# A two-branch encoder layer on one core: when branch B's token copies are made, how branch B's outputs lie in DRAM, and which engine makes the low parts of h's sums

## The chip, the cores and the metric

The kernel runs on one core of a Trainium2 chip. The core has a matrix engine (PE, TensorE; its weight loads are listed apart as PEld), a vector engine (DVE, VectorE), an activation engine (ACT, ScalarE), a general engine (POOL, GpSimd) and a queue that issues the DMAs (SP, SyncE). Each engine works off its own list of instructions in order; semaphores hold one back until its inputs are there. The metric is device time of one execution, in microseconds, as the median of several executions.

## The reference

An encoder layer with two parallel gated branches is applied to two requests with shared weights: a prompt of 512 tokens and a sample of 1024 tokens, 1024 channels each.

```python
h = rmsnorm(x, norm_g)
qa, ka, va, za, qb, kb, vb, zb, ga, gb = split(h @ w_in)
oa = neighbourhood_attention(rmsnorm(qa), rmsnorm(ka), va, rpb_a) * silu(za) @ w_o_a
ob = window_gqa_attention(rmsnorm(qb), rmsnorm(kb), vb, t5_table, sink) * silu(zb) @ w_o_b
y = x + (sigmoid(ga) * oa + sigmoid(gb) * ob) @ w_out
```

Branch A attends on a grid of 64 columns, 8 heads. Branch B attends to tokens at most 128 positions away, with 8 query heads on 2 key heads. All is in float32.

## The kernel before

**Precision.** Every operand of a large product is split in two parts for PE: a high part (ACT copies it into float32r) and a low part (the operand less its high part, on DVE or POOL). A product is then three matmuls: high by high, high by low, low by high (L1293 to L1295; L764 in the projections). The function split (L1168) makes both parts: the high part with ACT alone (L1172), the low part (L1177) with the choice any_tt, DVE or POOL.

**Stages.** For each request: norm, attention (attention_phase, L651), then the dense part (dense_phase, L1139): the paths z_a and z_b, the gates, the two branch projections and the output projection. The prompt runs first and the sample second; the sample's norm lies beside the prompt's dense part. In the trace the prompt's attention takes up to about 220 us, its dense part to about 400, the sample's attention to about 785 and its dense part the rest.

**The planner.** The kernel is first written as a list of operations, each with the engines that may do it and a price per engine, a due number (prio; small is early), the buffers that it needs, and the operations after which it comes. Flow.run (L207) then walks through time with these prices, gives each free engine the ready operation of the smallest due number, and so writes down each engine's order. An operation that DVE and POOL may both do is also marked port (L170): the planner starts it on one of them only when the other has no port operation running (barred, L252). The DMAs are priced by bytes alone (dma, L188). On the chip the engines follow these orders, and semaphores keep data right.

**Attention.** Tokens lie column by column of the grid. Branch A has four groups of two heads, branch B two groups of four; in each, project (L731) makes q, k and v of 128 tokens at a time (4 tiles in the prompt, 8 in the sample), with due number lead + t, lead being the group times the tiles. For branch B a tile is every nb-th token (nb = 4 or 8), so its operand is first copied together: hb, four copies of 128 x 512 for a tile (L751 to L757; ACT L665, DVE L667), in four buffers (HB). They are due one before their tile, and wait for all of h. f.begun (L775) holds the first matmul of each projection. Then sums of squares (ss, L788), rs_v and rs_r on POOL (L795, L802), the scaled q and k (qk, L819), transposes on PE (L864), scores, weights and outputs ot.

**Branch outputs.** Outputs go to DRAM (o_d, L404) and are read back when the path z is there (post_z, L1524). For branch B an output tile ot has 128 partitions: two parts e of 64 channels each, which the reader adds (L1540). Its store (L1098 to L1107) is two DMAs, one for each e: 64 partitions in runs of 128 tokens (512 B). The tokens of a row stand tile after tile in DRAM. The sample's reader takes a half of the tokens (L1532), so 64 tokens out of each of eight tiles, in runs of 256 B; the prompt's reader takes a whole row of 2 KB.

**Dense part.** Pairs of output blocks are made with sums of h and sums of weights (one level of Strassen's scheme, pair_strassen L1349), seven products in place of eight. The sample's sums of h are stored in DRAM (t_d) and loaded by stored_sums (L1236): sixteen tiles of 128 x 512, split into the tiles T. The same function loads the later sums of the merged branches (m_d). weight_tiles (L1260) splits the weights: whi by ACT, wlo by DVE or POOL; S are the sums of weights. The first z pair of a request has prio 0, the later ones 1 to 3. Filled gate products (fill_gates, L1592; fh, fl, fc, tile d) are put where PE has room.

Of the kernel before, what the change touches and what calls it, by code (L numbers as in the profile page):

```python
# [10 lines left out]
F32 = mybir.dt.float32  # L11
# [14 lines left out]
FILL_P, FILL_S = 3, 8  # L26
SLACK = 1.1
SCRATCH = 1024
CLASSIC_P = (4, 8, 4)
# [11 lines left out]
P = 128  # L41
# [313 lines left out]
def encoder_kernel(  # L355
# [23 lines left out]
    nc = tc.nc  # L379
# [23 lines left out]
    t_d = dpool.tile([4, 4, P, NT_S // 2], F32, tag="t_d", name="t_d")  # L403
    o_d = {geo.nt: dpool.tile([2, 8, P, geo.nt], F32, tag=f"o_d{geo.nt}", name=f"o_d{geo.nt}") for geo in (gp, gs)}  # L404

# [245 lines left out]
    def attention_phase(geo, hh, hl, h_ops, mask_d, early, late):  # L651
# [79 lines left out]
        def project(br, w, t, prio):  # L731
# [5 lines left out]
            if br == "A":  # L737
                hs = h_ops[t]
                part = [lambda k, v=v: v.t[:, k, t * P : (t + 1) * P] for v in (hh, hl)]
                held = [[hh] * KC, [hl] * KC]  # L740
                done = {}
            else:

                hs = []
                hb = [[tile_([P, KC // 2, P], F32R, "hb", HB) for _ in range(2)] for _ in range(2)]
                part = [lambda k, v=v: v[k // 4].t[:, k % 4] for v in hb]
                held = [[v[k // 4] for k in range(KC)] for v in hb]
                done = {}
                for q in range(2):
                    for m, v in enumerate((hh, hl)):  # L750
                        done[m, q] = f.op(  # L751
                            (("act", 960), ("dve", DVE_(512))),
                            lambda e, m=m, v=v, q=q: copy(
                                e, hb[m][q].t, v.t[:, 4 * q : 4 * q + 4, t:nt:nb].bitcast(F32)
                            ),
                            prio - 1, new=[hb[m][q]], hold=[v], after=[o for u in h_ops.values() for o in u], port=True,
                        )  # L757
# [79 lines left out]
        def over(v, runs):  # L837

            (a, n), b = runs[0], runs[-1][0]
            return v[:, a : a + n] if len(runs) == 1 else v.rearrange("p (a b) -> p a b", b=n)[:, a // n :: (b - a) // n]  # L840
# [120 lines left out]
        def weigh(br, gi, g, block, sums, pss, sbs, nb_t, info, prio):  # L961
# [114 lines left out]
            if br == "A":  # L1076
# [10 lines left out]
                def emit():  # L1087
                    if len(runs) == 1:
                        dst = over(o_d[nt][0, g], runs).rearrange("(i p) n -> p i n", i=2)
                        nc.sync.dma_start(dst, ot.t[:64, ::2])  # L1090
                        return
                    for i in range(2):
                        dst = over(o_d[nt][0, g, 64 * i : 64 * i + 64], runs)
                        nc.sync.dma_start(dst, ot.t[:64, 2 * i].rearrange("p (a b) -> p a b", b=64))

                stores[g, runs[0][0] // 512].append(sp(emit, 65536, prio, use=[ot]))
            else:
                for e in range(2):  # L1098
                    dst = o_d[nt][e, 4 + 2 * g : 6 + 2 * g, :, runs[0][0] : runs[0][0] + P]
                    dst = dst.rearrange("c (i d) n -> d (c i) n", d=64)  # L1100
                    o = sp(
                        lambda e=e, dst=dst: nc.sync.dma_start(dst, ot.t[e * 64 : e * 64 + 64]),
                        131072, prio, use=[ot],
                    )
                    for c in (4 + 2 * g, 5 + 2 * g):
                        for n in range(nt // 512):
                            stores[c, n].append(o)  # L1107

# [30 lines left out]
    def dense_phase(geo, hh, hl, h_ops, o_stores, exps_done, start, opened, tp, up, p0, p1, p2, x_t, y_t, classic, fill, after_gates=None, side=None):  # L1139
# [27 lines left out]

        def split(hi, lo, src, n, prio, new_hi, new_lo, src_v, after=()):  # L1168

# [5 lines left out]
            b = f.op(  # L1175
                any_tt(n),
                lambda e: engines[e].tensor_tensor(lo(), src(), hi().bitcast(F32), op=ALU.subtract), prio,  # L1177
# [58 lines left out]
        def stored_sums(prio, d, after):  # L1236

            tv, ops = {}, {}
            for j in (1, 2, 0, 3):
                tv[j] = tuple(f.value(tp, [P, 4, nh], F32R, "T", 8) for _ in range(2))  # L1240
                vh, vl = tv[j]
                for k in range(4):
# [6 lines left out]
                        lambda vh=vh, k=k: vh.t[:, k], lambda vl=vl, k=k: vl.t[:, k], lambda st=st: st.t[:, :nh], nh, prio,  # L1249
                        (vh, k == 0), (vl, k == 0), [st],  # L1250
                    )
# [7 lines left out]

        def weight_tiles(operands, per, prio):  # L1260

# [4 lines left out]
            for i, src in enumerate(operands):  # L1266
                at, q = [], 0
                while q < 4:
# [6 lines left out]
                        lambda src=src, sc=sc: src.t[:, sc], m * P, prio,  # L1275
                        (hi, ti not in seen), (lo, ti not in seen), [src],
                    )
# [71 lines left out]
        def pair_strassen(srcs, post, prio, mov_h, mov_t, seed=None, last=False, kept=None):  # L1349
# [10 lines left out]
            first = [] if kept else [raw[0, 0], raw[0, 1]]  # L1360
            w = weight_tiles([*first, s2, s3, s1, raw[1, 1], s4], 6, prio - 0.5)
            w = [None] * (7 - len(w)) + w
# [161 lines left out]
        def post_z(c, a, n, v, in_psum, prio):  # L1524
# [3 lines left out]
            for e, ot in enumerate(ots):  # L1528
                if c < 4:
                    src, dst = o_d[nt][e, c, :, a : a + n], lambda ot=ot: ot.t[:, :n]  # L1530
                else:
                    src = o_d[nt][e, c].rearrange("p (i n) -> p i n", n=P)[:, :, a // nb : a // nb + m]  # L1532
                    dst = lambda ot=ot: ot.t[:, :n].rearrange("p (i n) -> p i n", n=m)
                dma(
                    lambda dst=dst, src=src: nc.sync.dma_start(dst(), src), 512 * n, prio - 0.5, new=[ot],
                    after=o_stores[c, a // nh],
                )
# [416 lines left out]
```

## Time and profile before

| | us |
|---|---|
| median of 3 runs | 1136.02 |
| lowest and highest of them | 1134.59, 1136.24 |
| the profiled execution, as timed | 1135.29 |
| its span, first to last instruction | 1133.5 |

| engine | busy in the prompt's attention at 100 to 120 us | in the sample's attention at 500 to 520 | in the sample's dense part at 900 to 920 |
|---|---|---|---|
| PE | 20.00 | 20.00 | 20.00 |
| DVE | 15.98 | 16.23 | 13.12 |
| ACT | 16.82 | 12.21 | 7.94 |
| POOL | 8.98 | 12.38 | 6.32 |

Each stretch is 20 us long. Busy is the time in which an instruction of that engine runs; of the matmuls the ends are modelled, and consecutive ones overlap, so a PE that is busy throughout can still hold fewer matmuls than fit. The number of matmuls of a stretch therefore says more than its busy time. In the views an operation is named by its line, its engine and out<-in by the program's names; what stands behind an arrow is what ended the idle time ahead of it.

### The profile page before, as it was taken

The page shows a single profiled execution, that of the slowest core. Times are in us where ns is not written, and L with a number is a line of the kernel's source. Part 1 is how long each engine was busy: PE and PEld are TensorE (multiplying, and loading weights), DVE is VectorE, ACT ScalarE, POOL GpSimd, SP SyncE. Part 2 cuts the span into 40 slices and gives each one's busy share as a digit, 9 for nine tenths or more (in the row PEclk, how much of TensorE's full clock was granted, in tenths as well). Part 3 has the DMA queues.
Part 4 walks back from the last instruction along what each step waited for, and adds up shares of the span by engine and source line. Part 5 has one row for each costly group of instructions (what it writes and reads, how often), then busy time and mean ns, then how long its engine had stood idle before and what let it go on. Part 6 is the DMA issues. An engine that isn't in the chain of part 4 may idle for free.

```text
span 1133.5 us, 18690 instructions
## 1 busy us (share of the span) xinstructions
PE 1119.0 (99%) x6079; PEld 973.2 (86%) x6079; DVE 860.1 (76%) x1988; ACT 651.9 (58%) x1499; POOL 337.3 (30%) x438
## 2 busy tenths in 40 slices
PE   8999999999999999999999999999999999999998
PEld 6999988888888889999999988988788888888887
DVE  5888797587776568787878888885988766677764
ACT  6777987644432257565769888876543335423430
POOL 4653433000011154434324344420333322222211
PEclk9999999999999999999999999999999999999999
DMA  7854543488886732121212314244977645867862
GB/s 263 276 155 138 184 115 103 110 257 248 256 278 216 254 128 91 27 63 30 82 41 85 81 38 112 57 131 121 307 241 234 224 156 170 281 207 222 280 215 93
DMA packets 139108, 186.11 MB, mean 164 GB/s; under 512 B 29897, under 2 KB 68561, under 8 KB 139010
## 3 DMA queue, kind: packets, MB, share of 16 engines
q1 hardware_dynamic: 139010, 184.91, 51.8%
q8 instruction: 48, 0.79, 0.3%
q14 instruction: 50, 0.41, 0.1%
HBM read 137.66 MB, written 51.92 MB: 167 GB/s over the span
## 4 chain that ended last, share of the span: by engine, by line
PE 93%; DMA 2%; DVE 2%; issue 1%; ACT 1%; POOL 1%; SPq 0%; DVEq 0%; ACTq 0%
PE p L764 25%; PE x L1294 9%; PE x L1295 9%; PE x L1293 9%; PE x L1066 5%; PE x L937 5%; PE x L1029 5%; PE d L1293 4%; PE d L1295 4%; PE d L1294 4%; PE p L1294 4%; PE p L1295 4%; PE p L1293 4%; PE x L864 2%; DMA w<-in_w_att_dram 1%
## 5 line engine op out<-in xcount | busy, mean ns | idle before, releaser
L764 PE MATMUL p<-whi,hh 128*128 128x384 f32 x384 | 133.4, 348 | 0.0
L764 PE MATMUL p<-whi,hl 128*128 128x384 f32 x384 | 132.2, 344 | 0.0
L764 PE MATMUL p<-wlo,hh 128*128 128x384 f32 x384 | 131.8, 343 | 0.0
L1172 ACT ACTIVATE whi<-raw 128x512 fp32r<-128x512 f32 (+1 forms) x140 | 81.4, 600 | 71.2 <-PE x L1294 22.3
L981 ACT ACTIVATE sb<-sb,mx 128x384 f32<-128x384 f32 (+1 forms) x192 | 107.8, 565 | 16.9 <-DVE mx L972 16.5
L1295 PE MATMUL x<-T,wlo 128*128 128x512 f32 x280 | 108.9, 389 | 0.0
L1294 PE MATMUL x<-T,whi 128*128 128x512 f32 x280 | 108.9, 389 | 0.0
L1293 PE MATMUL x<-T,whi 128*128 128x512 f32 x280 | 108.9, 389 | 0.0
L764 PE MATMUL p<-whi,hb 128*128 128x384 f32 x384 | 107.6, 346 | 0.0
L1177 POOL TENSOR_TENSOR wlo<-raw,whi 128x512 fp32r<-128x512 f32 (+1 forms) x33 | 39.5, 1204 | 215.6 <-DMA raw<-in_w_g_dram 112.9
L1040 DVE TENSOR_TENSOR pp<-x,pp 128x512 fp32r<-128x512 f32 (+1 forms) x136 | 82.5, 638 | 19.6 <-ACT pp L1035 19.0
L1177 DVE TENSOR_TENSOR wlo<-raw,whi 128x512 fp32r<-128x512 f32 (+1 forms) x107 | 72.0, 682 | 32.3 <-ACT whi L1172 28.7
L802 POOL TENSOR_TENSOR rs_r<-rs_v,mhalf 128x4 f32<-128x4 f32 (+1 forms) x72 | 80.5, 1118 | 5.7
L1035 ACT ACTIVATE pp<-x 128x512 fp32r<-128x512 f32 (+1 forms) x136 | 70.8, 559 | 15.8 <-PE x L1029 14.3
L1294 PE MATMUL x<-hl,whi 128*128 128x512 f32 x200 | 77.8, 389 | 0.0
L1295 PE MATMUL x<-hh,wlo 128*128 128x512 f32 x200 | 77.8, 389 | 0.0
L1293 PE MATMUL x<-hh,whi 128*128 128x512 f32 x200 | 77.8, 389 | 0.0
L1066 PE MATMUL x<-pp,v 128*128 128x256 f32 (+1 forms) x368 | 75.8, 322 | 0.0
L764 PEld LDWEIGHTS p<-whi,hl 128*128 128x128 f32 x384 | 72.6, 189 | 1.3 <-issue 1.0
L764 PEld LDWEIGHTS p<-wlo,hh 128*128 128x128 f32 x384 | 72.7, 189 | 1.0 <-issue 0.7
L764 PEld LDWEIGHTS p<-whi,hh 128*128 128x128 f32 x384 | 72.7, 189 | 0.7 <-DVE v L812 0.3
L764 PEld LDWEIGHTS p<-whi,hb 128*128 128x128 f32 x384 | 69.1, 188 | 3.1 <-issue 1.3
(388 smaller groups left out, 2965.1 us busy)
## 6 DMA issues: line engine op xcount, KB each, us to landing
raw<-in_w_g_dram SPq DMA_DIRECT2D x84, 256.0 KB
w<-in_w_att_dram SPq DMA_DIRECT2D x46, 384.0 KB
raw<-in_w_z_dram SPq DMA_DIRECT2D x40, 256.0 KB
ot<-o_d SPq DMA_DIRECT2D x36, 256.0 KB
g_d<-C SPq DMA_DIRECT2D x34, 256.0 KB
fr<-in_w_g_dram SPq DMA_DIRECT2D x28, 256.0 KB
raw<-in_w_out_dram SPq DMA_DIRECT2D x28, 256.0 KB
out_dram<-C SPq DMA_DIRECT2D x19, 256.0 KB
```

What stands on the lines that cost most here:

```text
L764: pe.matmul(ps.t[:, :GW], part[u](k), mv.t[:, c], start=k == 0 and m == 0, stop=k == KC - 1 and m == 2,)
L802: lambda e: nc.gpsimd.tensor_tensor(r.t[:, :nn], rv.t[:, :nn], mhalf[:, :nn], op=ALU.pow),
L937: pe.matmul(pss[2 * pair + i].t[:, :width], q.t[rows, u, at : at + P], kv[:, tiles[0] : tiles[-1] + 1 : step], start=n == 0, stop=n == 2,)
L981: act.activation(sb.t[:, :width], sb.t[:, :width], AF.Exp, bias=mx.t[:, i : i + 1], scale=-1.0, accum_out=sm.t[:, i : i + 1],)
L1035: lambda e, pt=pt, pp=pp, nn=nn: act.activation(pp.t[:, 0, :nn], pt.t[:, :nn], AF.Copy),
L1040: lambda e, pt=pt, pp=pp, nn=nn: dve.tensor_tensor(pp.t[:, 1, :nn], pt.t[:, :nn], pp.t[:, 0, :nn].bitcast(F32), op=ALU.subtract),
L1066: pe.matmul(out(), v.t[:, vs], mv(), start=first, stop=last)
L1172: (("act", ACT_(n)),), lambda e: act.activation(hi(), src(), AF.Copy), prio,
L1177: lambda e: engines[e].tensor_tensor(lo(), src(), hi().bitcast(F32), op=ALU.subtract), prio,
L1293: pe.matmul(out, hi.t[:, cs], mh(), start=first and k == 0, stop=False, **more)
L1294: pe.matmul(out, hi.t[:, cs], ml(), start=False, stop=False, **more)
L1295: pe.matmul(out, lo.t[:, cs], mh(), start=False, stop=last and k == len(ws) - 1, **more)
```

## The change

Three things change. First, the copies hb of branch B's tokens also come after the first matmul of the projection six tiles back (AHEAD). Second, branch A's outputs keep o_d, now without the part e, and branch B's get a tensor of their own, ob_d: for each half of 512 tokens, eight blocks of 128 rows. A store takes all 128 partitions of ot for one half (two DMAs in the sample, with 64 tokens of a row each; one in the prompt, with 128), and a reader takes rows of 512 tokens. Third, split has a switch, both: where it is off, the low part has DVE alone. It is off for the sums of h that the sample loads (stored_sums with t_d), and for the weights of a Strassen pair with prio 0.

```diff
@@ -25,6 +25,7 @@
 ROTA = "ppxxxxxd"
 FILL_P, FILL_S = 3, 8
 SLACK = 1.1
+AHEAD = 6
 SCRATCH = 1024
 CLASSIC_P = (4, 8, 4)
 SIDE = {5: 0, 8: 1, 11: 2, 15: 3}
@@ -401,7 +402,8 @@
         rpb_x[geo.nt] = dpool.tile([8, P, 3 * geo.cw * 16], F32, tag=f"rpb_x{geo.nt}", name=f"rpb_x{geo.nt}")
     r_d = dpool.tile([NT_S // P, P], F32, tag="r_d", name="r_d")
     t_d = dpool.tile([4, 4, P, NT_S // 2], F32, tag="t_d", name="t_d")
-    o_d = {geo.nt: dpool.tile([2, 8, P, geo.nt], F32, tag=f"o_d{geo.nt}", name=f"o_d{geo.nt}") for geo in (gp, gs)}
+    o_d = {geo.nt: dpool.tile([4, P, geo.nt], F32, tag=f"o_d{geo.nt}", name=f"o_d{geo.nt}") for geo in (gp, gs)}
+    ob_d = {geo.nt: dpool.tile([geo.nt // 512, 8, P, 512], F32, tag=f"ob_d{geo.nt}", name=f"ob_d{geo.nt}") for geo in (gp, gs)}
 
     s_d = dpool.tile([4, 4, P, 512], F32, tag="s_d", name="s_d")
     s_saves = {}
@@ -753,7 +755,8 @@
                             lambda e, m=m, v=v, q=q: copy(
                                 e, hb[m][q].t, v.t[:, 4 * q : 4 * q + 4, t:nt:nb].bitcast(F32)
                             ),
-                            prio - 1, new=[hb[m][q]], hold=[v], after=[o for u in h_ops.values() for o in u], port=True,
+                            prio - 1, new=[hb[m][q]], hold=[v], port=True,
+                            after=[*(o for u in h_ops.values() for o in u), f.begun[nt, prio - AHEAD]],
                         )
             for k in range(KC):
                 hi, lo = w[k // 2]
@@ -1086,25 +1089,23 @@
 
                 def emit():
                     if len(runs) == 1:
-                        dst = over(o_d[nt][0, g], runs).rearrange("(i p) n -> p i n", i=2)
+                        dst = over(o_d[nt][g], runs).rearrange("(i p) n -> p i n", i=2)
                         nc.sync.dma_start(dst, ot.t[:64, ::2])
                         return
                     for i in range(2):
-                        dst = over(o_d[nt][0, g, 64 * i : 64 * i + 64], runs)
+                        dst = over(o_d[nt][g, 64 * i : 64 * i + 64], runs)
                         nc.sync.dma_start(dst, ot.t[:64, 2 * i].rearrange("p (a b) -> p a b", b=64))
 
                 stores[g, runs[0][0] // 512].append(sp(emit, 65536, prio, use=[ot]))
             else:
-                for e in range(2):
-                    dst = o_d[nt][e, 4 + 2 * g : 6 + 2 * g, :, runs[0][0] : runs[0][0] + P]
-                    dst = dst.rearrange("c (i d) n -> d (c i) n", d=64)
+                m, t = 512 // nb, runs[0][0] // P
+                for n in range(nt // 512):
+                    dst = ob_d[nt][n, 4 * g : 4 * g + 4, :, t * m : t * m + m].rearrange("a p m -> p a m")
                     o = sp(
-                        lambda e=e, dst=dst: nc.sync.dma_start(dst, ot.t[e * 64 : e * 64 + 64]),
-                        131072, prio, use=[ot],
+                        lambda n=n, dst=dst: nc.sync.dma_start(dst, ot.t[:, :, n * m : n * m + m]), 2048 * m, prio, use=[ot],
                     )
                     for c in (4 + 2 * g, 5 + 2 * g):
-                        for n in range(nt // 512):
-                            stores[c, n].append(o)
+                        stores[c, n].append(o)
 
         f.slack = SLACK
         groups = [("A", 0), ("A", 1), ("A", 2), ("A", 3), ("B", 0), ("B", 1)]
@@ -1165,7 +1166,7 @@
             choice = (("dve", DVE_(n)),) if psum else any_tt(n)
             return f.op(choice, lambda e: engines[e].tensor_tensor(out(), in0(), in1(), op=op), prio, **kw)
 
-        def split(hi, lo, src, n, prio, new_hi, new_lo, src_v, after=()):
+        def split(hi, lo, src, n, prio, new_hi, new_lo, src_v, after=(), both=True):
 
             kw = lambda v, new: {"hold": [v]} if new is None else {"new": [v]} if new else {"into": [v]}
             a = f.op(
@@ -1173,7 +1174,7 @@
                 use=src_v, after=after, **kw(*new_hi),
             )
             b = f.op(
-                any_tt(n),
+                any_tt(n)[: 1 + both],
                 lambda e: engines[e].tensor_tensor(lo(), src(), hi().bitcast(F32), op=ALU.subtract), prio,
                 use=src_v, after=[a, *after], **{**kw(*new_lo), "hold": [new_hi[0], new_lo[0]]},
             )
@@ -1247,7 +1248,7 @@
                     )
                     ops[j, k] = split(
                         lambda vh=vh, k=k: vh.t[:, k], lambda vl=vl, k=k: vl.t[:, k], lambda st=st: st.t[:, :nh], nh, prio,
-                        (vh, k == 0), (vl, k == 0), [st],
+                        (vh, k == 0), (vl, k == 0), [st], both=d is m_d,
                     )
             return moving_sums(tv, ops)
 
@@ -1257,7 +1258,7 @@
             dma(lambda: nc.sync.dma_start(v.t, src), 262144, prio, new=[v], after=[start])
             return v
 
-        def weight_tiles(operands, per, prio):
+        def weight_tiles(operands, per, prio, both=True):
 
             n = -(-len(operands) * 4 // per)
             his = [f.value(wpool, [P, 768], F32R, "whi", 6) for _ in range(n)]
@@ -1273,7 +1274,7 @@
                     ops = split(
                         lambda hi=hi, cols=cols: hi.t[:, cols], lambda lo=lo, cols=cols: lo.t[:, cols],
                         lambda src=src, sc=sc: src.t[:, sc], m * P, prio,
-                        (hi, ti not in seen), (lo, ti not in seen), [src],
+                        (hi, ti not in seen), (lo, ti not in seen), [src], both=both,
                     )
                     seen.add(ti)
                     at += [(hi, lo, (c + j) * P, ops) for j in range(m)]
@@ -1358,7 +1359,7 @@
                     new=[out], use=[in0, in1],
                 )
             first = [] if kept else [raw[0, 0], raw[0, 1]]
-            w = weight_tiles([*first, s2, s3, s1, raw[1, 1], s4], 6, prio - 0.5)
+            w = weight_tiles([*first, s2, s3, s1, raw[1, 1], s4], 6, prio - 0.5, prio > 0)
             w = [None] * (7 - len(w)) + w
             here = isinstance(kept, Value)
             p1 = kept if here else tile_("U", 4, sn)
@@ -1527,12 +1528,11 @@
             ots = [tile_("ot", n_ot) for _ in range(2 if c >= 4 else 1)]
             for e, ot in enumerate(ots):
                 if c < 4:
-                    src, dst = o_d[nt][e, c, :, a : a + n], lambda ot=ot: ot.t[:, :n]
+                    src = o_d[nt][c, :, a : a + n]
                 else:
-                    src = o_d[nt][e, c].rearrange("p (i n) -> p i n", n=P)[:, :, a // nb : a // nb + m]
-                    dst = lambda ot=ot: ot.t[:, :n].rearrange("p (i n) -> p i n", n=m)
+                    src = ob_d[nt][a // nh, 2 * c - 8 : 2 * c - 6, e * 64 : e * 64 + 64, :n]
                 dma(
-                    lambda dst=dst, src=src: nc.sync.dma_start(dst(), src), 512 * n, prio - 0.5, new=[ot],
+                    lambda ot=ot, src=src: nc.sync.dma_start(ot.t[:, :n], src), 512 * n, prio - 0.5, new=[ot],
                     after=o_stores[c, a // nh],
                 )
             ot, ov, sv = ots[0], lambda: ots[0].t[:, :n], lambda: sg.t[:, :n]
```

## The prediction, made before the changed kernel ran

> **What bounds the kernel now.** I read the page's header first, then who waited for whom on PE, then the stretches, then the timeline at the places that these point to.
>
> ```profile
> span 1133.5 us, 18690 instructions
> PE 1119.0 (99%) x6079; PEld 973.2 (86%) x6079; DVE 860.1 (76%) x1988; ACT 651.9 (58%) x1499; POOL 337.3 (30%) x438
> PE x L1811 <- DMA rb<-in_norm_row_dram: 4.4, 1, 4.4
> PE x L864 <- DVE qk L819: 3.1, 3, 1.8
> PE d L1294 <- DVE T L1177: 1.6, 1, 1.6
> PE p L1294 <- DVE T L1177: 0.9, 2, 0.7
> 20.00:40.00 20.00, 19.48 (x120) 17.04 (x119) 16.74 (x46) 13.06 (x27) 16.08 (x22) 1.00 0.76 251
> 400.00:420.00 20.00, 18.16 (x108) 16.65 (x107) 13.72 (x41) 9.29 (x22) 10.66 (x15) 1.00 0.42 140
> 786.00:806.00 20.00, 20.00 (x90) 16.57 (x89) 14.54 (x25) 13.76 (x26) 0.00 (x0) 1.00 0.96 296
> 806.00:821.00 15.00, 12.52 (x51) 9.07 (x50) 14.44 (x17) 7.04 (x14) 8.26 (x6) 1.00 0.94 299
> ```
>
> (Stretches: length, busy time and count of PE, PEld, DVE, ACT, POOL, then granted clock, DMA share, GB/s.) PE is the bound: 1133.5 - 1119.0 = 14.5 us idle in the whole span. The change can win only idle time of PE, and only what its three edits touch. The largest idle piece, 4.4 us, is the start's load of the norm row, which no edit touches. Two pieces are within reach. One lies at 400 to 420 (20.00 - 18.16 = 1.84 us). The other lies at 806 to 821: a full stretch holds 90 matmuls in 20 us, 0.222 us each, so 15 us should hold 67.5 and hold 51; 16.5 x 0.222 = **3.7 us** lost, of which 15.00 - 12.52 = 2.5 us show as idle (some records may be missing, so I use 2.5 to 3.7). In that stretch DVE is busy 14.44 of 15 us, and the DMA engines 0.94.
>
> **Part 1, the copies of h for branch B.** The rows are those of the tile hb (first two, and the last: who waited for it) and the timeline of the sample attention's start, where the first four copies stand:
>
> ```profile
> L665 ACT ACTIVATE hb<-hl x2: 1151/1156/1162, 31.8 to 32.9; 128x512 fp32r<-128x512 f32 x2
> L764 PE MATMUL p<-whi,hb x80: 331/336/447, 600.3 to 636.8; 128*128 128x384 f32 x80
> 402.04 2.46 ACT L665 ACTIVATE hb<-hh 128x512 fp32r<-128x512 f32 x2
> 402.23 1.31 POOL L1177 TENSOR_TENSOR fl<-fr,fh 128x512 fp32r<-128x512 f32 x1 [11.40 <-ACT fh L1172]
> 402.62 2.15 DVE L667 CAST hb<-hl 128x512 fp32r<-128x512 f32 x2
> 403.62 1.22 POOL L795 TENSOR_SCALAR rs_v<-ss 128x4 f32<-128x4 f32 x1
> 404.92 1.01 POOL L802 TENSOR_TENSOR rs_r<-rs_v,mhalf 128x4 f32<-128x4 f32 x1
> 405.97 0.42 DVE L819 TENSOR_TENSOR qk<-p,rs_r 128x256 f32<-128x256 f32 x1 [0.75 <-POOL rs_r L802]
> 406.02 0.19 POOL L795 TENSOR_SCALAR rs_v<-ss 128x4 f32<-128x4 f32 x1
> 406.45 0.44 PE L864 MATMUL x<-ident,qk 128*128 128x128 f32 x2 [1.84 <-DVE qk L819]
>   PEld p L764: 0.2, 1
> ```
>
> The matmuls on these copies begin at 600.3, so at 402 nobody needs them. They matter since POOL's rs_v takes 1.22 us beside the DVE casts, where the next rs_v takes 0.19, and rs_v, rs_r, qk and the transposes of L864 follow one another. Without the casts, rs_v costs 0.19: 1.22 - 0.19 = 1.03 us, all of it ahead of the PE instruction that waited 1.84 us. POOL's fl (1.31) still stands ahead of rs_v; if the order puts it on the freed DVE, up to 1.84 go. Bounds 0 to 1.84; I take **1.0**, the measured stretch.
>
> Only the first four copies of each request are gated in effect: the four buffers hold one tile, so later copies wait for the tile before, and the first matmul six projections back is long past by then. In the prompt the same four stand around 32 (first row); PE idles 20.00 - 19.48 = 0.52 us in all of 20 to 40, so at most 0.5 is to be won there, and as that idle time has other releasers I take 0.
>
> The gate puts the four beside the third tile of the third A group (prompt, 16 - 6 = 10) and of the fourth (sample, 32 - 6 = 26), tens of us before use. They wait in the planner, not in a queue, since an engine's order is written after its times are planned; no DMA moves. What they cost there: at most another 1.03 each if a cast meets an rs_v with PE's work just behind (2.1 together); at least 0. The nearest row is the 88 other copies that already run in the midst of B's tiles: all that PE's side ever waited for a copy is the last line, 0.2 us. I take 0.
>
> **Part 2, branch B's outputs by halves.** The sample's reads of B (1024 runs of 256 B each, eight per partition) become 128 rows of 2 KB; the prompt's reads were whole rows already.
>
> ```profile
> 791.26 0.41 SPq L1520 DMA_DIRECT2D u_d<-C  x1
> 791.71 2.14 SPq L1535 DMA_DIRECT2D ot<-o_d  x2
> 793.90 3.66 SPq L1520 DMA_DIRECT2D u_d<-C  x1
> 799.60 0.69 DVE L1166 TENSOR_TENSOR ot<-ot 128x512 f32<-128x512 f32 x1 [1.00 <-DMA ot<-o_d]
> 803.14 1.41 SPq L1535 DMA_DIRECT2D ot<-o_d  x2
> 804.60 3.58 SPq L1520 DMA_DIRECT2D u_d<-C  x1
> 803.77 6.24 DMA ot<-o_d
> 810.10 1.25 DVE L1166 TENSOR_TENSOR ot<-ot 128x512 f32<-128x512 f32 x1 [0.46 <-DMA ot<-o_d]
> L1102 SPq DMA_DIRECT2D o_d<-ot__9385 x2: 580/580/580, 702.5 to 703.4; - x2
> 720.00:740.00 20.00, 20.00 (x130) 18.08 (x129) 18.00 (x52) 17.01 (x45) 10.81 (x16) 1.00 0.16 42
> ```
>
> (The row without an engine is from the chain of waits, the last two from the tile o_d and the stretches.) Two pairs of such reads stand in the stretch before the stall. After each, SP's next store takes 3.66 and 3.58 us to issue instead of 0.41, and the loads of h's sums queue behind it. DVE waits 1.00 and 0.46 us for the reads themselves, and the chain of waits carries the second for 6.24 us. A read landing 1 us sooner ends both waits: **1.46 us** of DVE time, of the engine that PE waits for next. How much sooner is not shown: at most the 3.2 us of a stalled issue per pair; at least nothing, since the DMA engines are full anyway. I take enough to end the waits.
>
> The other side is the stores. The sample's two per tile go from 64 partitions in runs of 512 B to 128 partitions in runs of 256 B; the prompt's two become one (one issue of 0.58 less, off the path). An issue costs 0.58 now; afterwards between 0.41 (whole rows) and 1.07 (half of 2.14), so SP gains 0.3 or loses 1.0 us per tile, in B's attention, where PE waits for no DMA. The page "DMA: Bandwidth & Descriptors" of the Trainium skill (Specifications) speaks against this part: below 512 B a transfer does a read-modify-write. If that doubled the stores' engine time, they would still fit beside a share of 0.16 (last row above), and the sum would stay; no run here shows stores of 256 B.
>
> **Part 3, low parts on VectorE alone.** The timeline of the stretch that stalls:
>
> ```profile
> 807.79 1.30 POOL L1177 TENSOR_TENSOR T<-fh,T 128x512 fp32r<-128x512 f32 x1 [31.89 <-DVE wlo L1177]
> 808.37 1.27 DVE L1177 TENSOR_TENSOR T<-U,T 128x512 fp32r<-128x512 f32 x1
> 809.05 1.75 POOL L1177 TENSOR_TENSOR wlo<-S,whi 128x512 fp32r<-128x512 f32 x1
> 810.76 1.71 POOL L1177 TENSOR_TENSOR wlo<-raw,whi 128x512 fp32r<-128x512 f32 x1
> 811.27 1.75 DVE L1177 TENSOR_TENSOR T<-w,T 128x512 fp32r<-128x512 f32 x1
> 813.08 0.50 PE L1294 MATMUL d<-T,whi 128*128 128x512 f32 x1 [1.57 <-DVE T L1177]
> 818.77 1.29 POOL L1166 TENSOR_TENSOR S<-raw 128x512 f32<-128x512 f32 x1 [1.01 <-DMA raw<-in_w_z_dram]
> 818.84 1.78 DVE L1177 TENSOR_TENSOR T<-w,T 128x512 fp32r<-128x512 f32 x1
> 820.67 0.50 PE L1294 MATMUL p<-T,whi 128*128 128x512 f32 x1 [0.65 <-DVE T L1177]
> ```
>
> An operation of this size takes 0.69 us on DVE alone (799.60 above) and 1.27 to 1.78 beside a POOL operation. POOL's two wlo belong to the second pair (due 0.5), which keeps both engines, as do the sums S. The first pair's own weights (due 0) lose POOL too, but their low parts lie in 786 to 806, where POOL ran nothing. So of sixteen low parts of the sums the edit moves just one, the first row: DVE gets 0.69 more, and loses the 1.27 - 0.69 = 0.58 that this one cost it. Net **0**. What I cannot read off: operations with one engine are no longer held by the planner until POOL's shared-port work is done, so more of them may meet a POOL operation. Bounds: the two other slow rows here at 0.69 again, 1.06 + 1.09 = -2.2; six more of the rest slowed so, 6 x 1.09 = +6.5. I take 0, what the one shown move gives.
>
> The page "SBUF — State Buffer" of the Trainium skill (Who interferes with whom) says why: a VectorE operation with two SBUF inputs and a GpSimd operation that reads SBUF share a port that one holds to its end. By that rule the edit is worth nothing while POOL keeps other work; the rows above agree.
>
> **The sum.** Part 1: -1.0. Parts 2 and 3: DVE's chain comes 1.46 sooner, so the 2.5 to 3.7 us lost shrink by at least that; the loads of the last sums also leave the queue sooner, which can take the rest. DVE stays nearly full (14.44 of 15), so I stay near the lower end: **-2.0**. The profiled execution took 1135.29, 1.79 beyond its span and 0.73 below the median of 1136.02. 1135.29 - 3.0 = 1132.3; with the 0.73, **1132.9 us**.
>
> **Rivals.** (a) Both stalls go whole: 1.84 + 3.7 = 5.5 less, 1130.5; for it speaks that a DVE in order passes every lost us on. (b) DVE's rate, not the reads, holds the last sums: only the 1.0 of part 1, 1135.0; for it speaks DVE's 14.44 of 15 in the stall. (c) The change does not do what it says: the copies stop another rs_v for 1.03 and POOL takes other work beside the low parts, 1136.0. (d) Slower: the unheld low parts meet POOL. Each more meeting costs 1.09 on a DVE that PE already waits for; from the third on they cost more than the 1.0 + 1.46 won, and six give 1136.0 - 2.5 + 6.5 = 1140.0. For it speaks the planner's lost hold; against it that POOL's other work stays as it is.
>
> **Chances.** Forecast 0.48 (own range 1131 to 1134.6), (a) 0.14, (b) 0.18, (c) 0.10, (d) 0.10. A measurement of this kernel tells about 0.2%, 2.3 us, from no change: faster is below 1133.7. That holds 0.40 of the forecast's 0.48 and (a): 0.54; same 0.08 + 0.18 + 0.10 = 0.36; slower 0.10. The range, 1130.0 to 1137.0, leaves out a third of (a) and of (c), and (d): 0.18.
>
> **What would show it.** Right: no copy of h at 402, rs_v 0.19 there, PE's wait at L864 under 1 us; no SP issue over 1 us after B's reads, no DVE wait for them, over 56 matmuls in the 15 us of the first pair's sums. Wrong: more low parts slowed beyond 1.2 us than now, or a new PE wait near the copies' new place.

## The result, and the profile after

| | before | after |
|---|---|---|
| median, measured together (us) | 1134.59 (1133.55 to 1136.24, 5 runs) | 1223.31 (1222.05 to 1224.38, 5 runs) |
| ratio, 95% interval | | 1.0777 [1.0762, 1.0793] |
| the profiled execution, its span (us) | 1135.29, 1133.5 | 1224.38, 1222.6 |

The change costs 7.8%, where the forecast had a gain of 0.3%. The page's header of after, with the share of PE and the clock that PE was granted in 40 slices:

```profile
span 1222.6 us, 18683 instructions
PE 1144.3 (94%) x6079; PEld 987.3 (81%) x6079; DVE 853.4 (70%) x1967; ACT 649.4 (53%) x1500; POOL 355.4 (29%) x458
PEclk9999999987998999999999999998997699999999
```

The span grew by 89.1 us, and PE's two numbers divide it. PE's idle time went from 14.5 to 1222.6 - 1144.3 = 78.3 us, 63.8 more. The same 6079 matmuls were busy for 1144.3 - 1119.0 = 25.3 us longer: the clock dips in slices 9, 10 and 13 (30.6 us each, so 245 to 306 and 367 to 397), and again in 28, 31 and 32 (825 to 856 and 917 to 978). All lie in the dense parts of the prompt and of the sample, and all but slice 13 where the outputs of branch B are read back; in slice 13 the dip follows a wait of 2.54 us for hh (387.21). Who waited for whom, on PE and then on DVE (us in total, times, longest):

```profile
PE x L1296 <- DVE wlo L1178: 22.4, 3, 9.9
PE p L1296 <- DVE wlo L1178: 17.9, 3, 7.4
PE x L1294 <- ACT whi L1173: 12.0, 2, 11.0
PE x L1294 <- ACT T L1173: 5.2, 1, 5.2
```

```profile
DVE ot L1167 <- DMA ot<-ob_d: 90.5, 11, 11.1
```

PE waits for parts of weights and of sums. These stand behind the one instruction on which DVE waits: 90.5 us, in 11 waits, for the reads of branch B. The timeline of one of them, first SP's queue (x2: two issues in one row), then DVE, then PE (start, length, instruction, idle time ahead of it):

```profile
234.56 1.72 SPq L1535 DMA_DIRECT2D ot<-ob_d  x2
248.20 2.09 SPq L1535 DMA_DIRECT2D ot<-ob_d  x2
```

```profile
247.48 0.69 DVE L1167 TENSOR_TENSOR ot<-ot 128x512 f32<-128x512 f32 x1 [8.54 <-DMA ot<-ob_d]
261.22 0.69 DVE L1167 TENSOR_TENSOR ot<-ot 128x512 f32<-128x512 f32 x1 [7.47 <-DMA ot<-ob_d]
```

```profile
264.12 0.79 PE L1296 MATMUL p<-hh,wlo 128*128 128x512 f32 x1 [7.18 <-DVE wlo L1178]
264.71 0.63 PE L1294 MATMUL p<-hh,whi 128*128 128x512 f32 x1
265.14 0.63 PE L1295 MATMUL p<-hl,whi 128*128 128x512 f32 x1
...
267.54 0.39 PE L1295 MATMUL p<-hl,whi 128*128 128x512 f32 x1
267.77 0.39 PE L1296 MATMUL p<-hh,wlo 128*128 128x512 f32 x1
```

A pair of reads, 256 KB each, is issued from 248.20 and is there at 261.22, 13.0 us later. A pair of the prompt in before takes 5.9 us:

```profile
255.36 1.44 SPq L1535 DMA_DIRECT2D ot<-o_d  x2
261.23 0.69 DVE L1166 TENSOR_TENSOR ot<-ot 128x512 f32<-128x512 f32 x1 [2.33 <-DMA ot<-o_d]
```

The pair of the sample that the prediction shows took 7.0 us from its first issue (803.14 to 810.10). Behind the stall the matmuls come 0.43 us apart instead of 0.23 for about 3 us. Such stretches make up most of the 25.3 us: busy time times the missing clock, in stretches of 2 us, adds up to about 21 us (an estimate from this trace). Why a read takes 13 us, the stretches show (length, busy time and count of PE, PEld, DVE, ACT, POOL, then clock, DMA share, GB/s):

```profile
255.50:261.00 5.50, 1.45 (x7) 0.87 (x5) 0.00 (x0) 0.00 (x0) 0.00 (x0) 0.95 0.13 51
261.20:268.60 7.40, 4.48 (x13) 3.58 (x14) 5.95 (x9) 2.15 (x4) 0.00 (x0) 0.59 0.26 71
302.00:320.00 18.00, 18.00 (x81) 14.91 (x80) 11.63 (x28) 6.57 (x13) 0.00 (x0) 1.00 0.83 254
```

In the first, every engine runs out of work and only the reads are on their way. The DMA engines are then busy at 0.13, which is 2 of 16, and move 51 GB/s, where other transfers of the same kernel run at 254. A pair, 524288 bytes, takes 10.3 us at 51 GB/s. The read's source is ob_d[..., 2c-8 : 2c-6, e*64 : e*64+64, :n]: two blocks of 64 rows, so the outermost dimension of the access pattern has size 2. Before, it had the 128 rows outermost.

### The profile page after: what moved, and what is told of

It reads as the page before. It is cut to its first block, busy times and chain, and to the rows that moved or that the text cites. A ratio compares the mean times of both kernels' runs of the same rounds, so it can differ in the third digit from the quotient of the medians.

```text
span 1222.6 us, 18683 instructions
## 1 busy us (share of the span) xinstructions
PE 1144.3 (94%) x6079; PEld 987.3 (81%) x6079; DVE 853.4 (70%) x1967; ACT 649.4 (53%) x1500; POOL 355.4 (29%) x458
## 5 line engine op out<-in xcount | busy, mean ns | idle before, releaser
L1294 PE MATMUL x<-T,whi 128*128 128x512 f32 x280 | 112.9, 403 | 17.2 <-ACT whi L1173 12.0
L1296 PE MATMUL x<-T,wlo 128*128 128x512 f32 x280 | 112.6, 402 | 15.9 <-DVE wlo L1178 15.8
L1295 PE MATMUL x<-T,whi 128*128 128x512 f32 x280 | 112.3, 401 | 1.1 <-DVE T L1178 1.1
L1294 PEld LDWEIGHTS x<-T,whi 128*128 128x128 f32 x280 | 54.9, 196 | 30.0 <-ACT whi L1173 13.1
L1296 PEld LDWEIGHTS x<-T,wlo 128*128 128x128 f32 x280 | 54.5, 195 | 29.2 <-DVE wlo L1178 16.9
L1514 ACT ACTIVATE C<-C 128x512 f32<-128x512 f32 x38 | 23.8, 631 | 101.2 <-DVE C L1167 79.2
```

What stands on the lines that cost most here:

```text
L1294: pe.matmul(out, hi.t[:, cs], mh(), start=first and k == 0, stop=False, **more)
L1295: pe.matmul(out, hi.t[:, cs], ml(), start=False, stop=False, **more)
L1296: pe.matmul(out, lo.t[:, cs], mh(), start=False, stop=last and k == len(ws) - 1, **more)
L1514: (("act", ACT_(n)),), lambda e: act.activation(sg.t[:, :n], v.t[:, :n], fn), prio,
```

## The experiments

The theories ahead of the first four: **T1**, a DMA whose rows fall into two blocks runs on two of the 16 DMA engines; **T2**, the new order of the work (the gate, the low parts on DVE) makes the stalls; **T3**, the new places in DRAM or stores of 256 B are slow.

**Each read as two DMAs.** All three parts, but a read of branch B is issued as two DMAs of 64 rows.

```diff
-                dma(
-                    lambda ot=ot, src=src: nc.sync.dma_start(ot.t[:, :n], src), 512 * n, prio - 0.5, new=[ot],
-                    after=o_stores[c, a // nh],
-                )
+
+                def emit(ot=ot, src=src):
+                    for i in range(1 if c < 4 else 2):
+                        out = ot.t[:, :n] if c < 4 else ot.t[64 * i : 64 * i + 64, :n]
+                        nc.sync.dma_start(out, src if c < 4 else src[i])
+
+                dma(emit, 512 * n, prio - 0.5, new=[ot], after=o_stores[c, a // nh])
```

> All three parts of the change, but each read of branch B's outputs is two DMAs of 64 rows, one for each head, in place of one DMA of two blocks of 64 rows; both stand in one operation, so the planner's order is that of the changed kernel. Theory 1 (a DMA whose rows fall into two blocks is worked off by two of the 16 DMA engines): the reads land in 2 to 4 us instead of about 11, DVE's wait for them falls from 90 us to under 10, the time is 1129 to 1137 us. Theory 2 (the new order of the engines, from the gate on the copies or from the low parts, makes the stalls): 1210 to 1225 us, as the order is the same. Theory 3 (the new places in DRAM or the stores of 256 B are slow): 1200 us or more.

Measured: 1141.87 us against 1134.17 before on the same chip, ratio 1.0069 [1.0055, 1.0083]. DVE's wait for the reads in this kernel:

```profile
DVE ot L1167 <- DMA ot<-ob_d: 9.8, 7, 3.3
```

The same layout, the same stores, the same order of every engine's work: only the shape of the DMA differs, and 81 of the 89 us are gone. T2 and T3 fall for these. But T1 had 1129 to 1137, and about 7 us stay; and a pair lands 5.8 us after its first issue (255.07 to 260.91), about as in before, where T1 had 2 to 4.

**Parts 1 and 3, without part 2.** The kernel before with the gate and the switch both.

> The kernel before with the gate on the copies and the low parts on VectorE alone, and branch B's outputs as they were. Theory 1 (two engines for each read): 1130 to 1137 us. Theory 2 (the new order): over 1200 us. Theory 3 (places in DRAM): 1130 to 1137 us.

Measured: 1141.62 us, ratio 1.0064 [1.0050, 1.0079]. No large stall, so part 2 makes these; but some 7 us more than before here too, without any of part 2.

**Part 2 alone.**

> The kernel before with branch B's outputs by halves alone, reads as in the change. Theory 1 (two engines for each read): 1200 to 1235 us, with DVE's waits for these reads near 90 us. Theory 2 (the new order): 1130 to 1140 us. Theory 3 (places in DRAM, stores): 1200 us or more.

Measured: 1227.65 us, ratio 1.0826 [1.0798, 1.0854]. Part 2 carries the whole large loss.

**Two, four and eight blocks.** The kernel before, with branch B's outputs in DRAM as before but with a spare row after each 64, 32 or 16 rows, so that a read's 128 rows fall into so many blocks. The runs of 256 B and 512 B stay, and so does the order of every engine's work. The stores are cut at the blocks, so with four and eight blocks there are more of them. The read with two blocks:

```diff
-                    src = o_d[nt][e, c].rearrange("p (i n) -> p i n", n=P)[:, :, a // nb : a // nb + m]
+                    src = op_d[nt][e, c, :, :64].rearrange("b r (i n) -> b r i n", n=P)[:, :, :, a // nb : a // nb + m]
```

> The kernel before; only branch B's rows lie with one spare row behind each 64 in DRAM, so that a read's 128 rows fall into two blocks. Stores, their runs of 512 B, the planner's order and the reads' runs (256 B in the sample, 2 KB in the prompt) are those of before. Theory 1 (two engines for each read): 1200 us or more; the sample's reads, with 1024 runs of 256 B, are slower still than the change's, so up to 1300. Theory 2 and theory 3: 1133 to 1140 us.

> The kernel before with branch B's outputs laid out in DRAM with a spare row after each 32, so that a read's 128 rows fall into four blocks (two_blocks, with a spare row after each 64, took 1259.91 us). T1 (as many DMA engines as blocks): the DMA share of a stretch that holds such a read alone is 4/16 = 0.25 where two blocks show 0.13 and 51 GB/s, and the read's packets take half as long; of the two_blocks' 127 us that VectorE waits for these reads under 60 are left, and the time is 1138 to 1185 us. T3 (the new place in DRAM or the spare rows are slow as such): 1230 us or more, like two_blocks.

> The same with a spare row after each 16 rows, eight blocks. T1: eight DMA engines, and VectorE's waits for the reads come near the 7.7 us of the kernel before; as every other order of this kernel that was run took up to 7 us more than the kernel before, 1133 to 1145 us. T3: 1230 us or more.

| outermost size of the reads | us | ratio, 95% interval | DVE waits for the reads, us |
|---|---|---|---|
| 128 rows (before) | 1134.71 | 1 | 7.7 |
| eight blocks | 1157.59 | 1.0201 [1.0164, 1.0237] | 27.1 |
| four blocks | 1186.09 | 1.0452 [1.0424, 1.0480] | 60.5 |
| two blocks | 1259.91 | 1.1111 [1.1088, 1.1133] | 127.4 |

The last column is one row of DVE's waits for each of the four kernels, in the table's order:

```profile
DVE ot L1166 <- DMA ot<-o_d: 7.7, 7, 2.3
```

```profile
DVE ot L1169 <- DMA ot<-op_d: 27.1, 11, 3.3
```

```profile
DVE ot L1169 <- DMA ot<-op_d: 60.5, 11, 7.3
```

```profile
DVE ot L1169 <- DMA ot<-op_d: 127.4, 11, 14.5
```

A spare row that nobody reads costs 126 us (1259.91 against 1134.17 in its own runs), since it turns 128 rows into two blocks. From two to four to eight blocks the wait halves each time, which a rule "as many engines as blocks" asks for and T3 does not. The sizes were expected too low: four blocks lie 1 us above the range of T1, eight blocks 12.6 us above. What part the additional stores have in this was not measured. Short stretches that hold little but a read show the share of the DMA engines, one row each for two, four and eight blocks:

```profile
247.00:253.00 6.00, 6.00 (x28) 4.96 (x27) 0.00 (x0) 0.00 (x0) 0.00 (x0) 1.00 0.15 55
247.00:248.00 1.00, 1.00 (x7) 0.81 (x6) 0.00 (x0) 0.00 (x0) 0.00 (x0) 1.00 0.26 98
255.80:256.70 0.90, 0.90 (x6) 0.74 (x5) 0.90 (x4) 0.53 (x2) 0.00 (x0) 1.00 0.50 184
```

The shares are those of about 2, 4 and 8 of 16 engines, and the rate goes up with them, from 55 to 98 to 184 GB/s. This is T1 seen directly.

**What is left: each part alone.** **U1**: the other 7 us come from part 3, low parts that meet POOL's operations; **U2**: they come from part 1, the gate.

> The kernel before with part 1 alone (the copies of h for branch B wait for the projection six tiles back). Parts 1 and 3 together took 1141.62 us against 1134.17, 7.4 us more; in their trace PE waits at the sums of 809 to 824 us in pieces of 0.9 us, which the kernel before has only once. U1 (these come from part 3, low parts that meet GpSimd's operations): part 1 alone is free of them and takes 1132 to 1136 us. U2 (the gate shifts the whole later order and so makes them): 1139 to 1143 us.

> The kernel before with part 3 alone (low parts of h's sums and of the first pair's weights on VectorE alone, which the planner no longer holds back while GpSimd's shared-port work lasts). U1: 1138 to 1143 us, and in 805 to 826 us more low parts T of over 1.2 us on VectorE than the four of the kernel before, with PE waits of 0.9 us behind them. U2: 1132 to 1136 us, at most five such low parts.

> The kernel before with part 2 alone, each read of branch B as two DMAs of 64 rows. T1 (the two blocks are all that is wrong with part 2): the reads are 2 KB rows on all DMA engines, no read stalls SyncE for over 2 us, and the time is that of my forecast's part 2 without parts 1 and 3, 1131 to 1134 us. If 2 KB rows win nothing over runs of 256 B, or the stores of 256 B and the additional issue eat it: 1134 to 1137 us. Over 1138 us would mean that something of part 2 besides the blocks costs.

Measured, against 1134.95 before: part 1 alone 1138.76 us (1.0038 [1.0024, 1.0052]), part 3 alone 1138.93 (1.0035 [1.0022, 1.0048]), part 2 alone with reads apart 1138.87 (1.0038 [1.0024, 1.0052]). Neither U1 nor U2: three parts that have nothing in common cost 3.8 to 4.0 us each. Part 2's own expectation had said what over 1138 us would mean: something of part 2 besides the blocks costs. Part 1's trace shows an exchange at the place that it was meant for. POOL and DVE at the start of the sample's attention, and PE behind them:

```profile
404.70 0.19 POOL L797 TENSOR_SCALAR rs_v<-ss 128x4 f32<-128x4 f32 x1
```

```profile
408.58 1.49 DVE L699 TENSOR_TENSOR bias<-mask,raw 128x192 f32<-128x192 f32 x5 [1.94 <-DMA mask<-in_mask_s_dram]
410.00 0.41 DVE L821 TENSOR_TENSOR qk<-p,rs_r 128x256 f32<-128x256 f32 x1
```

```profile
406.58 0.38 PE L866 MATMUL x<-ident,qk 128*128 128x128 f32 x2
410.47 0.44 PE L866 MATMUL x<-ident,qk 128*128 128x128 f32 x2 [1.90 <-DVE qk L821]
```

The first transposes no longer wait. But DVE now waits 1.94 us at the bias for the load of the mask; qk stands behind it on DVE, and PE waits 1.90 us four microseconds later. SP's issue of that load and DVE's bias in before, and the issue in part 1 alone:

```profile
400.76 1.39 SPq L674 DMA_DIRECT2D mask<-in_mask_s_dram  x1
406.51 1.50 DVE L698 TENSOR_TENSOR bias<-mask,raw 128x192 f32<-128x192 f32 x5
```

```profile
402.29 1.32 SPq L675 DMA_DIRECT2D mask<-in_mask_s_dram  x1
```

DVE comes to the bias hardly later than before (406.64 against 406.51), while the load is issued 1.53 us later. So the load came late; it is not shown that the copies had covered it.

**Part 3 with the planner's hold.** The low parts on DVE alone, but still held until POOL's port operations end (port=True).

```diff
-                lambda e: engines[e].tensor_tensor(lo(), src(), hi().bitcast(F32), op=ALU.subtract), prio,
+                lambda e: engines[e].tensor_tensor(lo(), src(), hi().bitcast(F32), op=ALU.subtract), prio, port=True,
```

> Part 3 alone, but the planner still holds each low part until GpSimd's shared-port work ends. H1 (the lost hold is what costs): the low parts lie between GpSimd's operations again, 1132 to 1137 us. H2 (the load is what costs: VectorE has one operation more, and GpSimd takes other work in its place): 1138 to 1143 us, as without the hold.

Measured: 1135.52 us, ratio 1.0007 [0.9993, 1.0022]: as H1 has it, and the only kernel of its kind that stays level with before. Of the low parts T on DVE at 805 to 826, those over 1.2 us are four before, six in part 3 alone and two here. The 95% intervals of the two kernels only touch, 3.4 us apart in their medians.

**Part 1 with other distances.** AHEAD 10 and 4.

> Part 1 alone with the copies gated ten projections back instead of six (they then stand at another place of the same tiles). With six, part 1 alone took 1138.76 us against 1134.95: the first four copies left the start of the sample's attention, as forecast, but VectorE then waited 1.94 us there for the mask's load, and PE's wait at the same place stayed (1.9 us). N1 (that exchange, and the new order behind every edit, is what part 1 gives): again a wait for the mask or for GpSimd's rs_r of 1 to 2 us there, and 1134 to 1141 us. N2 (six is a bad place for the copies themselves, which would have to show as PE waits beside them at 80 to 146 us): 1131 to 1134 us.

> The same with the copies gated four projections back. N1: 1134 to 1141 us, with a wait of 1 to 2 us at the start of the sample's attention. N2: 1131 to 1134 us.

Measured: 1145.06 us (1.0110 [1.0071, 1.0148]) and 1140.83 (1.0049 [1.0029, 1.0068]). N2 falls. Ten lies 4 us above what N1 had, and with four PE's wait at that start shrank to pieces of 0.42 and 0.82 us, so N1 is not right in detail either; with ten PE waits 1.64 us there, behind rs_r, as N1 had. Six is no worse than the other two places, and all three give a kernel slower than before.

**Nothing changed but an estimate.** **R**: any new order costs, because the planner's order in the kernel before is a good one among those it can give; **P**: each part costs by itself. Each of three kernels is the one before with one number of the planner changed by about 1% or less, which reaches the chip only through the order.

```diff
-SLACK = 1.1
+SLACK = 1.105
```

```diff
-        return self.op((("sp", 470),), lambda e: emit(), prio, lag=nbytes / 360, **kw)
+        return self.op((("sp", 475),), lambda e: emit(), prio, lag=nbytes / 360, **kw)
```

```diff
-                        dma_free = max(dma_free, now + ns + 650) + got.lag
+                        dma_free = max(dma_free, now + ns + 655) + got.lag
```

> The kernel before, unchanged but for the planner's estimate: SLACK 1.105 in place of 1.1, so that another order is written, with no operation added, removed or bound. R (any new order costs, because the order of the kernel before is a good one among those that the planner can give): the three such kernels lie at 1135 to 1146 us, most of them at 1138 or above, like the parts alone (1138.76, 1138.93, 1138.87 us). P (parts 1, 2 and 3 each cost something of their own): the three lie at 1132 to 1137 us.

> The kernel before with the planner's estimate of a DMA issue at 475 ns in place of 470, nothing else. R: 1135 to 1146 us. P: 1132 to 1137 us.

> The kernel before with the planner's estimate of a DMA's start at 655 ns in place of 650, nothing else. R: 1135 to 1146 us. P: 1132 to 1137 us.

Measured, against 1134.89: 1144.99 us (1.0080 [1.0064, 1.0096]), 1140.32 (1.0043 [1.0014, 1.0072]) and 1140.95 (1.0049 [1.0032, 1.0067]). All three lie in R's range and none in P's: kernels without any change of the work lose 5.4 to 10.1 us. PE's waits in the first of them:

```profile
PE x L864 <- DVE qk L819: 2.2, 4, 0.9
PE x L1293 <- ACT hh L1172: 2.1, 1, 2.1
PE x L1293 <- ACT fl L1648: 1.8, 1, 1.8
PE d L1293 <- ACT fc L1616: 1.4, 2, 0.7
```

The waits for hh and fl are new; those for qk and fc stand in before too, with 3.1 and 0.2. PE idles 1143.3 - 1124.6 = 18.7 us here against 14.5, and the same matmuls are busy 5.6 us longer; behind the waits for hh and fl the clock falls (see the last section).

Two things limit what R explains. The lists of instructions of the last two kernels are nearly the same (about 30 of PE's 6074 matmuls stand elsewhere), so the three are rather two new orders, and both are far from that of before (about 2200 elsewhere). And the parts change the order by very different amounts: part 1 alone moves about 800 matmuls, part 3 alone 15, part 2 with reads apart none (61 of DVE's 1988 operations, 17 of ACT's 1289). So R can account for part 1. For parts 2 and 3 it is not shown, and P is not excluded. Part 2's loss goes along with the clock: ten of its twelve executions have a mean granted clock of 0.997 or 0.998, where 15 of 64 executions of before are below 1.00 (0.998 or 0.999); its two at 1.00 took 1134.74 and 1136.82 us. Which wait brings the clock down there is open, since the profiled execution is one of those two.

**All parts, both faults mended.** Reads apart, and the hold kept.

> All three parts, with each read of branch B as two DMAs of 64 rows, and the low parts on VectorE alone held until GpSimd's shared-port work ends. Both faults found so far are mended; reads_apart, without the hold, took 1141.87 us, and the hold took 3.4 us off part 3 alone. If those 3.4 us come off here too: 1136 to 1140 us. If the rest is the new order's: 1138 to 1146 us. My forecast's gains, were they real and only hidden by the two faults: 1131 to 1134 us.

Measured: 1139.28 us, ratio 1.0037 [1.0024, 1.0051]: in both of the first two ranges, which overlap. Against its own before it is 4.4 us slower, where reads apart without the hold was 7.7 slower, and the two intervals lie apart. So the hold is worth 3.3 us here and 3.4 in part 3 alone; it moves about 24 of PE's matmuls each time. The kernel is below all three kernels without a change, but not where the forecast's gains would put it. No kernel here beats the one before.

## Why the prediction was wrong, step by step

**The step that failed is a bound in part 2**: how much sooner the reads land is "at least nothing, since the DMA engines are full anyway". They land 6 to 7 us later: 13.0 for a pair against 5.9 and 7.0 in before. The prediction counted "128 rows of 2 KB" and priced by the run length; it did not look at the access pattern that the DMA is given, whose outermost dimension went from 128 to 2. It also put the question to the sample only, since "the prompt's reads were whole rows already"; the prompt's four pairs stall as well (247.48, 261.22 and two more). The Trainium skill has the rule, in "DMA: Bandwidth & Descriptors", section "Why a DMA increments its semaphore by 16 and not by 1": the number of DMA engines is the largest up to 16 that divides the slowest dimension that isn't 1 on both sides. The trace agrees: a share of 0.13 at size 2, 0.26 at four and 0.50 at eight. Whether the stores of 256 B, for which the forecast cited another section of that page, cost anything is not shown: they are one of the things that differ in part 2 with reads apart, 3.9 us slower than before, and were not tried alone.

**The other forecasts of part 2.** With reads apart the stretch 806 to 821 holds 61 matmuls, over the 56 that were to show it right, where before held 51:

```profile
806.00:821.00 15.00, 14.04 (x61) 11.00 (x60) 14.51 (x19) 8.35 (x17) 7.08 (x5) 1.00 0.90 296
```

A stretch 2 us later holds 57, where before held 52. So the place could be won in part: PE waits there for T for 1.6 us in all, against 2.5. SP's next store behind the two pairs takes 0.53 and 0.50 us to issue where before took 3.66 and 3.58, as forecast, though the four reads of the first pair take 3.53 themselves, where two took 2.14. But the reads do not land sooner: 7.1 us for the second pair (804.40 to 811.50) against 7.0, and DVE waits 7.3 us for them in all against 7.7. That longer runs make the difference is therefore not shown.

**Part 1, -1.0.** The local reading was right: rs_v takes 0.19, and the first wait is gone. What the sum lacks is what would be late next: it was the mask's load, issued later in the new order, which gave back 1.90 us for the 1.84 won. In after itself PE's waits at that line fell from 3.1 to 1.7 us, since the order there differs again:

```profile
PE x L867 <- DVE qk L822: 1.7, 3, 1.0
```

**Part 3, 0.** Rival (d) saw that unheld low parts meet POOL more often, and they do, six for four. Its price, 1.09 us for each more, gives 2.2; with the hold back the kernel is 3.3 to 3.4 us faster. So the part cost more than the 0 that was taken.

**The missing rival.** That an edit can make the planner write another order far beyond the place that it is meant for, as part 1 does, was not among the cases at all. Twelve kernels other than before with reads on all engines lie at 1135.5 to 1145.1 us; eleven of them are more than 0.2% above before. Even had the layout been harmless, the time would have been above the range of 1130 to 1137: with reads apart all three parts took 1141.87. Why the order of before is better than these was not tried; nor was a kernel whose order is written from measured times.

**The bound itself** was read rightly: PE was the bound, and only its idle time could be won. That 14.5 us of idle time limits a gain says nothing about a loss. (The last step of the sum is off by 0.1: 1135.29 - 3.0 + 0.73 is 1133.0.)

## What to carry to other kernels

When a layout changes, write down the access pattern of every DMA that touches it, with the outermost dimension first, before counting run lengths: a block of two outside costs seven eighths of the DMA engines, and it is mended by one DMA for each block. Where a planner or a compiler writes the order, measure a change against some kernels with no change but a slightly different estimate; here those took 0.4 to 0.8% longer than the one before, and gains of 0.1 to 0.3% drown in that. Count, too, how many instructions the edit has moved: a small edit can move 800 matmuls or none. When a stall is removed, look up when the next load behind it is issued.

## What the hardware showed that was not expected

The granted clock can fall at a stall, and not only at a long one. After the stall of 7.18 us the stretch 261.2 to 268.6 has a clock of 0.59, with matmuls 0.43 us apart instead of 0.23. In the first kernel with nothing changed (SLACK), a wait of 1.83 us was followed by the same:

```profile
806.72 0.39 PE L1295 MATMUL x<-hh,wlo 128*128 128x512 f32 x1
808.93 0.50 PE L1293 MATMUL x<-hh,whi 128*128 128x512 f32 x1 [1.83 <-ACT fl L1648]
...
809.89 0.63 PE L1293 MATMUL x<-hh,whi 128*128 128x512 f32 x1
810.32 0.63 PE L1294 MATMUL x<-hl,whi 128*128 128x512 f32 x1
```

```profile
808.50:812.50 4.00, 3.57 (x10) 2.83 (x11) 4.00 (x8) 2.66 (x6) 0.00 (x0) 0.63 1.05 303
```

The other two kernels of that kind have the same wait of 1.83 us for the same fl, at 802.61 and at 802.12. The stretch behind it, with the estimate of the issue at 475 and of the landing at 655:

```profile
803.00:806.00 3.00, 3.00 (x9) 2.35 (x8) 3.00 (x7) 1.33 (x4) 0.00 (x0) 0.50 1.14 298
```

```profile
803.00:806.00 3.00, 3.00 (x15) 2.47 (x14) 3.00 (x7) 2.21 (x5) 0.00 (x0) 1.00 1.15 316
```

Nine matmuls against fifteen, behind waits of the same length: the length of a wait alone does not decide. What does was not tried. The Trainium skill, "TensorE: Matmul & The Clock Gate", section "Why this matters for your kernels", warns of gaps over about 3 us; here a shorter one was followed by 4 us at 0.63, by estimate 4 x 0.37 = 1.5 us lost, nearly the wait itself again.
